# Input projections of a hybrid decoder block: 2x2 block products with seven multiplications in place of eight

## The chip, the cores and the metric

The kernel runs on one core of one Trainium2 chip. The metric is the device time of one execution in microseconds (us); the time of a kernel is the median of its runs. A profiled execution gives, for one run, what each engine did when: TensorE (PE) for matmuls, VectorE (DVE), ScalarE (ACT) and GpSimd (POOL) for the rest, and SyncE (SP), whose queue issues most of the DMA transfers.

## The reference

One decoder block over 2048 positions of 1024 channels, in float32, cut to what matters here:

```python
u = rmsnorm(h, pre_g)                       # [2048, 1024]
z = u @ w_in                                # w_in is [1024, 8192]
xr, zr, q, k, v, za, gm = split(z)          # 1024 channels each, gm 2048
xc = causal_depthwise_conv(xr)              # 4 taps
y_r = rg_lru(xc) * silu(zr)                 # gated linear recurrence over the positions
o = diff_attention(q, k, v, lam)            # 8 heads, two softmaxes of 64 channels each, causal
y_a = rmsnorm(o) * silu(za)
g_r, g_a = split(sigmoid(gm))
m = g_r * (y_r @ w_br_rnn) + g_a * (y_a @ w_br_attn)
h = h + rmsnorm(m @ w_out, post_g)
```

The projection `u @ w_in` is 64 blocks of 128 output channels. Each product of two float32 matrices is done as three float16 matmuls: both sides are scaled by a power of two and split into a high and a low part, and high x high, high x low and low x high are summed in PSUM.

## The kernel before

The kernel has three stages, one after the other, with some overlap at the seams. It is written with a tile framework that adds the waits and puts each engine's instructions in an order by a model of their times, so neighbouring steps interleave.

**The input.** Sixteen tiles of 128 positions are loaded (L240), normalised (`x_stat`, `x_fin`, L252 to L277), split into float16 high and low parts on ACT and on DVE or POOL, and transposed by DMA (L276) into `uT`, which stays in SBUF until the end of attention.

**A weight block** (1024 x 128) is loaded (`w_load`, L145), its sum of squares taken (`w_stat`, L156), a power of two found by a tiny matmul and DVE steps (`w_scale`, L162 to L171), and split into high and low (`w_fin`, L177 on ACT, L178 on DVE). `mm3` (L187 to L194) multiplies a block with 512 positions: 8 parts of the contraction x 3 = 24 matmuls of 512 columns.

**LRU stage.** For each of 8 blocks of 128 channels and each half of the sequence (a half-row), `xr_half` and `zr_half` project x_r and z_r (4 chunks of 24 matmuls), then come the convolution (L324, L327), a split into two float32r parts (`xsplit`), the gate matmuls (`gates`, L351 to L353, twelve of 512 columns), and the recurrence with its scan (`gates2`, L376), then `fin` and `fin2` write the result to DRAM (L416).

**Attention stage.** The work of one head and 128 queries is a unit; there are 128. A unit computes scores (`a_scores`, L814), takes their maximum while DVE copies them out of PSUM (L826, L830), exponentials on ACT (`a_exp`, L851), combines the two softmaxes (`a_comb`, L874 on DVE, L876 on ACT, L877 on POOL), transposes the result by DMA (`pt`, L880), and two units later (`LAG`) multiplies it with v (`a_pv`, L897). Between the units stand groups of projection matmuls as filler, in an order written out as a list (`fills`, L743 to L770): k and q of a chunk (`g_k`, `g_q`, 24 matmuls each, whose outputs are split by `split16`, L667 and L668, and laid out by DMA from SBUF to SBUF, ten transfers a chunk), v and z_a (`g_va`, L711) and the merge gates (`g_gm`, L726 to L729, whose results go to DRAM). How many groups a unit gets is set by its size (L941 to L948).

**Branch stage.** The two branch products (L1094), the merge with the gates read back from DRAM (L1098 to L1108), the output projection (L1125) and the last norm.

## Time and profile before

| | us |
|---|---|
| runs of before: median (lowest to highest of 3) | 2504.65 (2502.78 to 2508.94) |
| span of the profiled execution, first to last instruction | 2506.1 |
| PE busy in it | 2353.1 |
| DVE busy in it | 1548.4 |
| ACT busy in it | 1224.6 |
| POOL busy in it | 679.7 |

The profiled execution has a span of 2506.1 us of its own; its own time with what lies around the span is not listed apart from the three runs, so the span is compared with their median. In a row of a group stands: line, engine, operation, what is written from what, shape and count, then the busy time of all of them together with the mean time of one in ns, then how long the engine was idle before them and who ended that idle time. Matmuls are pipelined: the listed 379 ns of one is longer than the distance from one to the next.

### The profile page before, as it was taken

Reading aid. Unit: us, or ns where it says so; the run is one execution under the profiler, and the core shown is the slowest. Engines: PE = TensorE matmul, PEld = TensorE weight load, DVE = VectorE, ACT = ScalarE, POOL = GpSimd, SP = SyncE. Lnnn points to the kernel's source line nnn. Section 1 sums busy time; section 2 is a strip of 40 time slices with the busy share of each in tenths; the row PEclk is TensorE's granted clock in tenths of the full one; section 3 lists DMA queues with packets and bytes.
Section 4 is the critical chain, followed back from the end, with each engine's and each line's share of the span. In section 5 each row is a group of like instructions: output and inputs, shape, how many; then the busy total and the mean of one; then the engine's idle time right before and its main releaser. Section 6 shows DMA issues by size and latency. Waiting matters only on the chain. (4 is left out here: it accounts for less than half of the span.)

```text
span 2506.1 us, 41430 instructions
## 1 busy us (share of the span) xinstructions
PE 2353.1 (94%) x15240; PEld 1355.3 (54%) x15240; DVE 1548.4 (62%) x4316; ACT 1224.6 (49%) x2156; POOL 679.7 (27%) x415
## 2 busy tenths in 40 slices
PE   6789999999998999998998999999999899999998
PEld 5344444465665665665665655655655444444443
DVE  8877667668658566667567478468467244633323
ACT  5555545456547546556456457356456244312211
POOL 3443334212222212222222222223123133322211
PEclk9899999999999999999999999999999999999999
DMA  9511111235444534635535445445445854743202
GB/s 244 104 43 48 46 42 34 76 81 119 108 96 111 113 84 108 127 82 113 115 84 114 103 96 118 95 90 124 95 90 115 251 177 135 239 148 118 84 17 101
DMA packets 541323, 268.73 MB, mean 107 GB/s; under 512 B 370504, under 2 KB 518016, under 8 KB 541120
## 3 DMA queue, kind: packets, MB, share of 16 engines
q1 hardware_dynamic: 538144, 256.74, 42.6%
q0 software_dynamic: 2816, 9.08, 1.2%
q8 instruction: 119, 1.95, 0.3%
q14 instruction: 84, 0.69, 0.1%
q10 hardware_dynamic: 160, 0.27, 0.0%
HBM read 110.79 MB, written 41.94 MB: 61 GB/s over the span
## 5 line engine op out<-in xcount | busy, mean ns | idle before, releaser
L192 PEld LDWEIGHTS <-w 128*128 128x128 f16 x5040 | 475.9, 100 | 576.5 <-issue 89.2
L192 PE MATMUL mm<-uT,w 128*128 128x512 f16 x3072 | 705.1, 383 | 12.9 <-ACT gm L728 8.9
L877 POOL TENSOR_TENSOR e<-e,e 128x1024 f16<-128x1024 f32 (+2 forms) x192 | 317.0, 1666 | 970.6 <-ACT e L876 487.0
L851 ACT ACTIVATE e<-e,nb,sc_h 128x1024 f32<-128x1024 f32 (+7 forms) x384 | 376.1, 980 | 160.8 <-DVE nb L845 125.6
L826 DVE TENSOR_SCALAR_CACHE_REDUCE e<-sc 128x1024 f32<-128x1024 f32 (+7 forms) x352 | 305.2, 880 | 134.9 <-PE sc L814 122.3
L192 PE MATMUL ps<-uT,w 128*128 128x512 f16 (+1 forms) x1968 | 354.4, 345 | 26.1 <-ACT xr L318 17.7
L711 PE MATMUL mm<-wva,uT 128*128 128x256 f16 x3072 | 352.7, 275 | 3.3 <-DVE st L668 2.6
L1094 PE MATMUL psb<-yt,w 128*128 128x512 f16 x1536 | 332.9, 379 | 2.0 <-ACT w L177 1.5
L711 PEld LDWEIGHTS <-uT 128*128 128x128 f16 x3072 | 301.5, 99 | 48.8 <-issue 2.9
L814 PE MATMUL sc<-K,Q 128*128 128x512 f16 (+3 forms) x1280 | 287.2, 351 | 19.9 <-DVE e L826 13.8
L897 PE MATMUL o<-V,pt 128*128 128x128 f16 x3264 | 224.5, 222 | 38.4 <-DMA pt<-e 38.1
L1094 PEld LDWEIGHTS <-w 128*128 128x128 f16 x1536 | 149.1, 98 | 184.9 <-issue 3.9
L897 PEld LDWEIGHTS <-pt 128*128 128x128 f16 x3264 | 200.0, 99 | 72.8 <-DMA pt<-e 46.5
L876 ACT ACTIVATE e<-e 128x1024 f16<-128x1024 f32 (+2 forms) x192 | 150.1, 802 | 143.1 <-DVE e L874 118.5
L814 PEld LDWEIGHTS <-Q 128*128 128x128 f16 x1280 | 119.6, 99 | 133.2 <-issue 20.2
L874 DVE SCALAR_TENSOR_TENSOR e<-e,rs,e 128x1024 f32<-128x1024 f32 (+2 forms) x192 | 190.0, 1017 | 2.2
L1125 PE MATMUL psf<-wo,m 128*128 128x512 f16 x720 | 155.7, 379 | 0.0
L156 ACT ACTIVATE jk<-wst 128x1024 bf16<-128x1024 f32 x80 | 84.2, 1052 | 138.7 <-DMA wst<-in_w_in_dram 102.6
L1125 PEld LDWEIGHTS <-m 128*128 128x128 f16 x768 | 75.1, 98 | 90.6
L1098 DVE SCALAR_TENSOR_TENSOR t<-gt,psb 128x512 f32<-128x512 f32 x64 | 43.8, 686 | 120.2 <-PE psb L1094 100.1
L1148 ACT ACTIVATE jk<-psf 128x1024 bf16<-128x1024 f32 x15 | 15.4, 1024 | 134.0 <-PE psf L1125 69.4
L717 DVE SCALAR_TENSOR_TENSOR V<-mm,V 128x256 f16<-128x256 f32 x64 | 26.9, 421 | 85.7 <-ACT V L716 85.6
(247 smaller groups left out, 2417.3 us busy)
## 6 DMA issues: line engine op xcount, KB each, us to landing
wst<-in_w_in_dram SPq DMA_DIRECT2D x64, 512.0 KB, 4.5
xt<-in_x_dram SPq DMA_DIRECT2D x32, 512.0 KB, 4.5
gm_d<-gm SPq DMA_DIRECT2D x64, 256.0 KB, 2.7
gt<-gm_d SPq DMA_DIRECT2D x32, 512.0 KB, 3.8
K<-st SPq DMA_DIRECT2D x128, 64.0 KB, 2.0
Q<-st SPq DMA_DIRECT2D x64, 128.0 KB, 2.4
Q<-st SPq DMA_DIRECT2D x128, 64.0 KB, 2.1
ya_d<-yT SPq DMA_DIRECT2D x64, 128.0 KB, 2.0
```

What stands on the lines that cost most here:

```text
L156: nc.scalar.activation(jk, w.st, AF.Square, accum_out=ss)
L192: nc.tensor.matmul(ps, w.t[:, a, k, :], uT[:, b, k, c0:c0 + n], start=(i == 0), stop=(i == 3 * KD - 1))
L711: nc.tensor.matmul(ps[:, j, :], uT[:, a, k, s0:s0 + 128], wt[:, b, k].rearrange("p t f -> p (t f)"), start=(i == 0), stop=(i == 3 * KD - 1))
L814: nc.tensor.matmul(ps[:, x * 128:x * 128 + m], Qt[h, t // 4][:, v, ci, q0:q0 + 128], K[:, ci, 0:m], start=(v == 0), stop=(v == 1))
L826: nc.vector.tensor_scalar(out=ev[:, 0:m], in0=ps[:, 0:m], scalar1=1.0, scalar2=None, op0=ALU.mult, op1=ALU.max, accum_out=u.mx[:, ci, col: ...
L851: nc.scalar.activation(ev[:, 0:nb * 128], ev[:, 0:nb * 128], AF.Exp, bias=nb_[:, ci:ci + 1], scale=sc_h[h], accum_out=u.sm[:, pi, ci:ci + 1])
L874: nc.vector.scalar_tensor_tensor(out=e0[:, 0:m], in0=e1v[:, 0:m], scalar=rs, in1=e0[:, 0:m], op0=ALU.mult, op1=ALU.add)
L876: nc.scalar.activation(e1[:, 0, 0:m], e0[:, 0:m], AF.Copy)
L877: nc.gpsimd.tensor_tensor(out=e1[:, 1, 0:m], in0=e0[:, 0:m], in1=e1[:, 0, 0:m], op=ALU.subtract)
L897: nc.tensor.matmul(o, pt[:, a, kb % 8, :], V[:, kb % 4, b, :], start=(kb == 0 and i == 0), stop=(kb == n - 1 and i == 2))
L1094: nc.tensor.matmul(ps, w.t[:, p, k, :], y_t[b][:, q, k, sl], start=(i == 0), stop=(i == 3 * KD - 1))
L1125: nc.tensor.matmul(pn[n], m16[:, a, j, ms], wo[:, b, j, ns], start=(j == 0 and a == 0 and b == 0), stop=(j == KD - 1 and a == 1))
```

## The change

Four k/q pairs (heads 0 to 3) are projected first, in the plain way: heads 0 and 1 in pieces of 128 positions as the x tiles arrive, heads 2 and 3 in chunks while further input tiles are built. Then come 14 pairs of blocks: x_r with z_r (L, 8 pairs), k with q of heads 4 to 7 (K), and gate blocks 12 to 15 (G, 2 pairs), in the order `S1_ORD`. A pair and half of the sequence form a group. The contraction (1024) is cut in two halves, the pair's two blocks are the two rows, and the half sequence's two chunks of 512 are the two columns of a 2x2 block product, which is done with seven products of 12 matmuls where plain blocks take eight (Winograd's form). For this four sums and differences of weight blocks (S1 to S4) are formed on POOL in each pair, and four of input blocks (T1 to T4) once: x is loaded a second time, combined on DVE and POOL, split and transposed again (`t_load`, `t_build`). Running sums stay in PSUM: bank Y is copied out by ACT (`ev`) before the next product adds to it, and three additions a group are made on DVE (`add_to`).

k and q go to DRAM (`kq_d`) and are loaded from there in attention, six transfers a chunk, four units ahead (`load_kq`). Two of the input's parts (`ub12`) go to DRAM and come back before attention. Attention keeps v, z_a and 12 gate blocks as filler; the first weights of attention are no longer prepared in the LRU stage under a list of their own. Weight blocks are held as two halves in a ring of 10 places (before: 4 whole blocks); some constants (`ACC0`, `SEG_B`, a scale exponent) change with it.

The core of the diff; removed lines are those of the old functions named above.

```diff
+S1_ORD = "L0 K4 L1 K5 L2 G6 L3 K6 L4 G7 L5 L6 L7 K7"
+NGM = 12
...
-        uT = utp.tile([128, 2, KD, S], F16, name="uT")
+        uK = [utp.tile([128, 2, 12, CH], F16, name=f"uK{p}") for p in range(2)]
...
+            pY = lx.enter_context(tc.tile_pool(name="pY", bufs=2, space=PSUM))
+            pX = lx.enter_context(tc.tile_pool(name="pX", bufs=1, space=PSUM))
+            pZ = lx.enter_context(tc.tile_pool(name="pZ", bufs=2, space=PSUM))
+            pG = lx.enter_context(tc.tile_pool(name="pG", bufs=3, space=PSUM))
...
+            def t_build(p, i, ts):
+                a, b = ts
+                for j, t in enumerate((a, b)):
+                    n = p * 8 + j * 4 + i
+                    nc.vector.scalar_tensor_tensor(out=t, in0=t, scalar=rx_t[:, n:n + 1], in1=gb,
+                                                   op0=ALU.mult, op1=ALU.mult)
+                sl = slice(i * 128, (i + 1) * 128)
+                h0, h1 = slice(0, CH), slice(CH, D)
+                nc.vector.tensor_tensor(out=a[:, h0], in0=b[:, h0], in1=a[:, h0], op=ALU.subtract)
+                nc.gpsimd.tensor_tensor(out=b[:, h0], in0=b[:, h1], in1=b[:, h0], op=ALU.subtract)
+                nc.vector.tensor_tensor(out=b[:, h1], in0=b[:, h1], in1=a[:, h0], op=ALU.subtract)
+                nc.vector.tensor_tensor(out=a[:, h1], in0=a[:, h1], in1=b[:, h1], op=ALU.subtract)
+                for src, k0 in ((a, 0), (b, 8)):
+                    u = x_tile(F16, [128, 2, D])
+                    nc.scalar.activation(u[:, 0], src, AF.Copy)
+                    (nc.gpsimd if k0 else nc.vector).tensor_tensor(out=u[:, 1], in0=src, in1=u[:, 0], op=ALU.subtract)
+                    for l in range(2):
+                        nc.sync.dma_start_transpose(out=uM[p][:, l, k0:k0 + 8, sl], in_=u[:, l])
...
+            def p_prep1(r):
+                for w, f in zip(r.w, r.fac):
+                    w_scale(w, gps(1), f)
...
+                nc.gpsimd.tensor_scalar(out=w0.st, in0=w0.st, scalar1=rt, scalar2=None, op0=ALU.mult)
+                r.q = {}
+                for nm, (w, k) in (("A11", (w0, 0)), ("A12", (w0, 4)), ("A22", (w1, 4))):
+                    r.q[nm] = wq_tile()
+                    split_w(r.q[nm], w.st[:, k:k + 4, :], w1.sg)
...
+            def p_prep2(r):
...
+                nc.gpsimd.tensor_tensor(out=a22, in0=a21, in1=a22, op=ALU.add)
+                nc.gpsimd.tensor_tensor(out=a21, in0=a11, in1=a21, op=ALU.subtract)
+                nc.gpsimd.tensor_tensor(out=a11, in0=a22, in1=a11, op=ALU.subtract)
+                nc.gpsimd.tensor_tensor(out=a12, in0=a12, in1=a11, op=ALU.subtract)
+                for nm, src in (("S2", a11), ("S1", a22), ("S3", a21), ("S4", a12)):
+                    r.q[nm] = wq_tile()
+                    split_w(r.q[nm], src, w1.sg)
...
+            def prod(ps, r, p, a, b, start, stop):
+                t, k0 = ublk(p, b)
+                q = r.q[a]
+                i = 0
+                for k in range(4):
+                    for x_, y_ in ((0, 0), (0, 1), (1, 0)):
+                        nc.tensor.matmul(ps, q[:, x_, k, :], t[:, y_, k0 + k, :], start=start and i == 0,
+                                         stop=stop and i == 11, skip_group_check=True)
+                        i += 1
+
+            def ev(src):
+                t = evp.tile([128, CH], F32, tag="Y", name="Y")
+                nc.scalar.activation(t, src, AF.Copy)
+                return t
+
+            def add_to(g, slot, ps, t):
+                dst = c_dst(g, slot)
+                nc.vector.tensor_tensor(out=dst, in0=ps, in1=t, op=ALU.add)
+                c_use(g, slot, dst)
+
+            def g_P1(g):
+                g.Y = pY.tile([128, CH], F32, tag="Y", name="psY")
+                prod(g.Y, g.r, g.p, "A11", "B11", True, True)
+                g.y1 = ev(g.Y)
+
+            def g_P56(g):
+                g.Z = pZ.tile([128, CH], F32, tag="Z", name="psZ")
+                prod(g.Z, g.r, g.p, "S1", "T1", True, True)
+                prod(g.Y, g.r, g.p, "S2", "T2", False, True)
+                g.u2 = ev(g.Y)
+
+            def g_P27(g):
+                X = pX.tile([128, CH], F32, tag="X", name="psX")
+                prod(X, g.r, g.p, "A12", "B21", True, True)
+                add_to(g, 0, X, g.y1)
+                prod(g.Y, g.r, g.p, "S3", "T3", False, True)
+                u3 = ev(g.Y)
+                add_to(g, 3, g.Z, u3)
+
+            def g_P43(g):
+                prod(g.Y, g.r, g.p, "A22", "T4", False, True)
+                c_use(g, 2, g.Y)
+                prod(g.Z, g.r, g.p, "S4", "B22", False, True)
+                add_to(g, 1, g.Z, g.u2)
...
+            for r in plain[2:]:
+                for c in range(NC):
+                    t_build(tn // 4, tn % 4, tl_n)
+                    tn += 1
+                    if tn < 8:
+                        tl_n = t_load(tn // 4, tn % 4)
+                    for f in range(2):
+                        g_plain(r, f, c)
...
+            g_P1(grps[0])
+            for g in grps:
...
+                if nxt:
+                    if g.p == 0:
+                        p_stat(nxt)
+                    else:
+                        p_prep2(nxt)
+                        if n + 2 < len(pairs):
+                            p_load(pairs[n + 2])
+                g_P56(g)
+                tick()
+                g_P27(g)
+                if nxt and g.p == 0:
+                    p_prep1(nxt)
+                if g.n + 1 < len(grps):
+                    g_P1(grps[g.n + 1])
+                tick()
+                g_P43(g)
...
+            def load_kq(h, c):
+                s0 = c * CH
                 t = kp.tile([128, 2, CH], F16, tag="K", name="K")
+                for l in range(2):
+                    nc.sync.dma_start(out=t[64 * l:64 * l + 64], in_=kq_d[0, h, l, :, s0:s0 + CH].rearrange(
+                        "(i p) s -> p i s", i=2))
...
             def chunk_groups(h, c):
-                return [("k", h, c), ("q", h, c), ("va", h, c, 0), ("va", h, c, 1)]
+                return [("va", h, c, 0), ("va", h, c, 1)]
 
-            gms = [("gm", f, c) for f in range(2 * NH) for c in range(NC)]
+            gms = [("gm", f, c) for f in range(NGM) for c in range(NC)]
```

The steps of the recurrence are the same, on the same engines; they are called one, two and three half-groups after their projection (`tick`).

More of the change, by code (lines that the diff above doesn't have):

```diff
@@ new lines, in u_sl, with mm3 @@
+            def u_sl(l, k, c0, n):
+                p, j, o = c0 // HALF, (c0 // CH) % 2, c0 % CH
+                if j == 0:
+                    return uK[p][:, l, k, o:o + n]
+                return uK[p][:, l, 4 + k, o:o + n] if k >= 4 else ub12[p][l][:, k, o:o + n]
+            def mm3(ps, w, c0, n):
+                i = 0
+                for k in range(KD):
+                    for a, b in ((0, 0), (0, 1), (1, 0)):
+                        nc.tensor.matmul(ps, w.at(a, k), u_sl(b, k, c0, n), start=(i == 0), stop=(i == 3 * KD - 1))
+                        i += 1
@@ new lines, with after, tick, c_dst @@
+            later = []
+            clock = [0]
+            def after(n, f):
+                later.append((clock[0] + n, f))
+            def tick():
+                clock[0] += 1
+                for e in [e for e in later if e[0] <= clock[0]]:
+                    later.remove(e)
+                    e[1]()
+            lru = {}
+            def c_dst(g, slot):
+                if g.r.kind == "L" and slot < 2:
+                    if slot == 0:
+                        lru["xr"] = lp.tile([128, HALF + 3], F32, tag="xr", name="xr")
+                    return lru["xr"][:, 3 + slot * CH:3 + (slot + 1) * CH]
+                return stp.tile([128, CH], F32, tag="C", name="C")
@@ L464 @@
             nc.vector.tensor_copy(out=prm, in_=prm_ps)
-            cw = [prm[:, KD * t:KD * (t + 1)] for t in range(4)]
             cb, ba, bx, ap_ = (prm[:, KD * t:KD * (t + 1)] for t in range(4, 8))
@@ new lines, with u_blk @@
+            while later:
+                tick()
+        ubp = utx.enter_context(tc.tile_pool(name="ubp", bufs=1))
+        ub12 = [ubp.tile([128, 2, 4, CH], F16, name=f"ub12{p}") for p in range(2)]
+        for p in range(2):
+            for l in range(2):
+                nc.sync.dma_start(out=ub12[p][:, l].rearrange("p k s -> p (k s)"), in_=b12_d[p, l])
+        def u_blk(l, k, s0, n=128):
+            p, c, o = s0 // HALF, (s0 // CH) % 2, s0 % CH
+            if c == 0:
+                return uK[p][:, l, k, o:o + n]
+            return uK[p][:, l, 4 + k, o:o + n] if k >= 4 else ub12[p][:, l, k, o:o + n]
@@ L594 @@
             ps_m = ax.enter_context(tc.tile_pool(name="ps_m", bufs=2, space=PSUM))
[L597 removed]
+            wl = {}
             wva_t = {}
```

712 lines of the change are left out of this document (387 added, 325 removed).

## Prediction

> **What bounds the kernel now.** I read the page first, for the span and the busy time of each engine, then a table by stage, then what TensorE (PE) waited for, and last the rows of single groups.
>
> ```profile
> span 2506.1 us, 41430 instructions
> PE 2353.1 (94%) x15240; PEld 1355.3 (54%) x15240; DVE 1548.4 (62%) x4316; ACT 1224.6 (49%) x2156; POOL 679.7 (27%) x415
> ```
>
> PE is busy for 94% of the span and idle for 2506.1 - 2353.1 = 153.0 us. The stages show where that idle time lies. The columns are window, length, busy time of PE, PE's weight loads, VectorE (DVE), ScalarE (ACT) and GpSimd (POOL), granted clock, DMA share and GB/s.
>
> ```profile
> 0.00:54.00 54.00, 29.52 (x396) 28.44 (x397) 42.56 (x125) 31.05 (x46) 12.26 (x16) 0.94 1.02 247
> 54.00:104.00 50.00, 35.66 (x290) 22.47 (x287) 46.80 (x92) 21.88 (x30) 27.61 (x20) 0.86 0.85 159
> 104.00:150.00 46.00, 39.27 (x174) 19.37 (x173) 36.84 (x64) 29.15 (x30) 17.54 (x8) 0.96 0.08 24
> 150.00:450.00 300.00, 285.92 (x1281) 138.95 (x1280) 212.36 (x247) 157.09 (x146) 109.94 (x60) 0.97 0.14 44
> 450.00:488.00 38.00, 33.91 (x150) 15.82 (x148) 25.77 (x35) 20.47 (x21) 12.69 (x7) 0.96 0.09 28
> ...
> 600.00:640.00 40.00, 35.08 (x242) 18.83 (x240) 37.20 (x101) 30.04 (x56) 13.97 (x7) 0.96 0.53 127
> ...
> 1963.00:2506.00 543.00, 523.46 (x2428) 236.68 (x2426) 209.98 (x531) 135.06 (x194) 136.29 (x78) 0.99 0.44 140
> ```
>
> ```profile
> 488.00:1963.00 1475.00, 1405.40 (x10532) 893.55 (x10533) 974.11 (x3227) 829.87 (x1692) 363.39 (x228) 0.98 0.49 106
> ```
>
> Idle PE time by stage: opening (0 to 104 us) 24.5 + 14.3 = 38.8; the rest of the LRU stage (104 to 488) 6.7 + 14.1 + 4.1 = 24.9; attention 1475 - 1405.4 = 69.6; branch stage 19.5. So every stage after the opening is bound by PE, and matmuls taken away there are worth their full time as long as nothing else becomes late. The reader should keep two rows. In the opening the DMA share is 1.02, so transfers set the pace. In 600 to 640, inside attention, DVE is busy for 37.20 of 40 us and PE only for 35.08: a stretch where DVE is the late one. PE's waits inside attention say the same:
>
> ```profile
> PE o L897 <- DMA pt<-e: 38.1, 30, 3.2
> PE sc L814 <- DVE e L826: 13.8, 9, 4.4
> ```
>
> PE waits for the transposed softmax weights, the end of a chain through DVE, ACT, POOL and DMA, and for DVE to empty the score banks.
>
> **Term 1: the matmuls removed.** A pair of blocks over half of the sequence took 2 blocks x 2 chunks x 24 = 96 matmuls of 512 columns; seven products of 12 are 84. There are 14 pairs x 2 halves = 28 groups, so 28 x 12 = 336 matmuls go. Their pitch where nothing disturbs PE is in the chain that ended last:
>
> ```profile
> 2249.07 165.76 PE psb L1094 x768
> ```
>
> 165.76 / 768 = 0.2158 us, and 336 x 0.2158 = 72.5 us, certain as long as PE is the bound. It is a small net of large moves: 16 k and q blocks and 4 gate blocks leave the attention stage, where they were the filler between units, and 4 plain pairs and 6 product pairs enter the first stage. The terms below are therefore changes of idle time, stage by stage.
>
> **Term 2: the opening.** Before, three half-rows were computed as x tiles arrived; now four k and q blocks over the whole sequence are, and two more pairs follow while the differences of the input (T1 to T4) are built.
>
> ```profile
> 17.95 0.26 PE L192 MATMUL ps<-uT,w 128*128 128x128 f16 x1 [2.90 <-DMA uT<-u]
> ```
>
> PE has 8 blocks x 96 x 0.2158 = 165.7 us of work here, from 18 us on, and then the first product group (84 x 0.2158 = 18.1 us) before the second half's T is needed: 202 us. The DMA has, from the shapes in the code: x 8.4 MB, its transposes 8.4, x again for T 8.4, T's transposes 8.4, k and q to DRAM 8.4, weights of six pairs 6.3, two of the input's parts to DRAM 2.1, the gain 0.5: 50.9 MB. At the first row's 247 GB/s and share 1.02, that is 242 GB/s at full share, 210 us: 8 us late. With 18 us of start and some 14 us of chain latency for the first T that makes 40 us idle against 38.8: **+1 us**. Bounds: nothing but the start idle, 20 us, is -19. At the second row's rate, 159 / 0.85 = 187 GB/s, the DMA takes 272 us, 70 us late: 90 us idle, +51. I take the first row's rate since its mix of loads and transposes is the nearer one.
>
> **Term 3: the product stage.** The gate matmuls of the LRU are unchanged in number; twelve of them lie between these two rows:
>
> ```profile
> 244.40 0.58 PE L351 MATMUL ps<-xh,gwh 128*128 128x512 f32 x1
> ...
> 247.40 7.94 PE L192 MATMUL ps<-uT,w 128*128 128x512 f16 x36
> ```
>
> 3.0 us a half-row. PE's work is 28 x 84 x 0.2158 + 16 x 3.0 = 556 us. At the idle share of 150 to 450, 14.08 / 300 = 4.7%, that gives 27 us idle. New is a tight hand-over: the running sum in bank Y is copied out by ACT before the next product may add to it, and two of the three copies in a group have only one product (12 x 0.2158 = 2.6 us) of other PE work ahead. The copy itself is like this row, and what ACT may be doing when it comes is like the other two:
>
> ```profile
> L667 ACT ACTIVATE st<-mm 128x512 f16<-128x512 f32 x64 | 37.6, 587 | 66.4 <-PE mm L192 57.3 <-PE tot L162 4.9 <-DMA Q<-st 3.2
> L156 ACT ACTIVATE jk<-wst 128x1024 bf16<-128x1024 f32 x80 | 84.2, 1052 | 138.7 <-DMA wst<-in_w_in_dram 102.6 <-POOL wst L150 30.1 <-DMA ya_d<-yT 5.6
> ```
>
> ```profile
> ACT sq L369 <- DVE sq L363: 31.0, 12, 4.9
> ```
>
> 0.59 us fits four times into 2.6 us; behind one long operation it still fits; but ACT stood up to 4.9 us at the head of its queue waiting for DVE's sq, and a copy behind that is late. ACT was busy 157.09 of 300 us, so most copies find it free: 56 hand-overs x 0.1 us = 6. Idle 33 against 24.9: **+8**. Bounds: none late, +2; each late by one ACT operation, 56 x 1.05 = 59, +61. The three additions a group (DVE, from PSUM) and the seven half-splits a pair hide beside the products; what they do to DVE is the fourth rival.
>
> **Term 4: into attention.** Before, head 0's k and q projections covered the preparation of its v and z weights, and PE's waits at the seam were short:
>
> ```profile
> 487.67 0.28 PE L711 MATMUL mm<-wva,uT 128*128 128x256 f16 x1 [0.60 <-ACT wva L177]
> ...
> 490.26 0.27 PE L814 MATMUL sc<-K,Q 128*128 128x128 f16 x1 [1.19 <-DMA Q<-st]
> ```
>
> ```profile
> wst<-in_w_in_dram SPq DMA_DIRECT2D x64, 512.0 KB, 4.5
> ```
>
> Now the first PE work of attention is v and z themselves, in tiles that stand where the first stage's lie; only the last group's products can cover them. If the loads are early, a split on ACT and DVE and its semaphores remain: **+4 us**. Bounds: 0 if all is covered; two loads of 4.5 us, a square of 1.05 and two splits behind the last product, some 13 us. The Trainium skill (TensorE: Matmul & The Clock Gate, Part 1) says that an idle window of about 3.4 us halves PE's clock; by it a seam of 4 us costs some 1.7 us more, an estimate from that page. The granted 0.86 of 54 to 104 us, beside 14.3 us of idle, agrees in kind.
>
> **Term 5: attention.** Its PE work falls by more than a quarter, DVE's hardly. The first two rows are those of the projection line L192 alone, in the attention window and behind it.
>
> ```profile
> 488.00:1963.00 1475.00, 657.76 (x2873) 279.31 (x2874) 0.98 0.49 106
> 1963.00:2000.00 37.00, 24.58 (x104) 10.48 (x102) 0.95 0.94 299
> ```
>
> ```profile
> L668 DVE SCALAR_TENSOR_TENSOR st<-mm,st 128x512 f16<-128x512 f32 x64 | 43.8, 685 | 54.9 <-ACT st L667 54.9
> ...
> L178 DVE SCALAR_TENSOR_TENSOR w<-wst,w_sg_agm,w 128x1024 f16<-128x1024 f32 x16 | 23.8, 1487 | 0.8 <-ACT w L177 0.7
> ```
>
> Of its 2873 matmuls there, 12 gate blocks keep 12 x 96 = 1152, less the 104 that run after 1963: 1048. So 1825 go; at 0.2158 they are 394 us, at their own 657.76 / 2873 = 0.229 they are 418, say 405: PE's 1405 becomes 1000. DVE loses the split of k and q (43.8) and 20 weight splits of 1.49 (30): 974 becomes 900. DVE's work over PE's goes from 0.69 to 0.90; in 600 to 640 it was 37.20 / 35.08 = 1.06, with PE idle for 4.92 of 40 us, 12.3%, where the stage as a whole idled for 69.6 / 1475 = 4.7%. I read the idle share off the straight line between these two: 4.7 + (0.90 - 0.69) / (1.06 - 0.69) x 7.6 = 9.0%, and 1000 x 0.09 / 0.91 = 99 us against 69.6: **+29**. Bounds: 4.7% gives 50 us, -20; 12.3% gives 140 us, +71.
>
> On the queues: before, SP issued ten copies a chunk that laid k and q out, behind their splits; now six loads from DRAM, issued four units ahead, and SP has less to issue between the transposes of the softmax weights. I cost this at nothing; without the lead it would be a wait like the 1.19 us above, once a chunk. The branch stage keeps its matmuls and its 19.5 us; its weight splits come in halves, behind PE: 0.
>
> **Sum.** -72.5 + 1 + 8 + 4 + 29 = -30.5, so 2506.1 - 30.5 = 2475.6 us in a profiled execution. The profiled execution of before was 1.5 us above the median of its runs, 2504.65; taken off, that is **2474 us**. With every term at its low end the changes add up to -110, with every term at its high end to +124.
>
> **Rivals.** *Everything hides* (2415 us): the hand-overs cost nothing and attention keeps 4.7%: -72.5 + 1 + 2 + 0 - 20 = -89.5. For it speaks that PE reached 95% of 1475 us already, against it the 600 to 640 row. Chance 0.15.
>
> *DVE paces attention* (slower). If the whole stage runs as 600 to 640 does, because too little filler lies between a unit's scores and its product with v, the idle time is 140 us and the sum 2474 + 71 - 29 = 2516 us. It decides from an idle share of 11.4%, where attention's idle time has grown by 60 us and the gain is gone. For it: the two waits quoted at the start, both on that chain; DVE would need 900 of 1140 us. Against it: the 40 us are one dense stretch, between quieter ones in which DVE catches up. Chance 0.15.
>
> *The opening waits for DMA* (2474 + 50 = 2524 us), if the transposes run at the second row's rate. Against it: in 54 to 104 us DVE was busy for 46.80 of 50 us and held up what the transposes read. Chance 0.07.
>
> *DVE paces the LRU groups*. In 150 to 450 us there were 1281 / 108 = 11.9 half-rows, so DVE had 212.36 / 11.9 = 17.9 us each. Three additions of the kind of the first row below (2.1 us) and three more half-splits a pair (0.9 a half-row) make 20.9 us, beside PE's 84 x 0.2158 + 3.0 = 21.1. POOL gets a scaling like the third row and four half-size additions and subtractions like the second for each pair, (1.86 + 4 x 1.20) / 2 = 3.3 us a half-row, and some DVE operations with two inputs in SBUF take far longer than their like: the fourth row has a median of 1282 ns and a longest of 3150 ns.
>
> ```profile
> L1098 DVE SCALAR_TENSOR_TENSOR t<-gt,psb 128x512 f32<-128x512 f32 x64 | 43.8, 686 | 120.2 <-PE psb L1094 100.1 <-PE tot L162 9.4 <-issue 4.7
> ...
> L1108 POOL TENSOR_TENSOR m<-t,m 128x512 f16<-128x512 f32 x32 | 38.5, 1204 | 116.5 <-ACT m L1107 116.5
> ...
> L324 POOL TENSOR_SCALAR xc<-xr,prm 128x1024 f32<-128x1024 f32 x16 | 29.7, 1859 | 56.7 <-ACT xr L318 53.3 <-DVE xt L266 3.3
> ```
>
> ```profile
> L327 DVE SCALAR_TENSOR_TENSOR xc<-xr,prm,xc x48: 1270/1282/3150, 73.4 to 456.6; 128x1024 f32<-128x1024 f32 x48
> ```
>
> If each new POOL operation holds DVE up for its whole length, a half-row takes DVE 24.2 us, 3.1 more than PE, and 16 of them 50 us: 2524. The Trainium skill (SBUF — State Buffer, Who interferes with whom) has it as a rule: a DVE instruction with two SBUF inputs and a GpSimd instruction that reads SBUF exclude each other, and whichever starts second waits for all of the other. The long ones of the fourth row would fit it; that POOL was the cause is not shown by this row. What speaks against the price is the order of the pairs: k/q and gate groups, which need DVE for about 8 of 18 us, stand between most LRU groups. Chance 0.05.
>
> *The change is not what it says*: fewer than 336 matmuls go. The page's count would show it; I give it no chance of its own, since the loops write out 84.
>
> **How the numbers follow.** My forecast, 2440 to 2497 us, has 0.50; an outcome between it and before, 2497 to 2512, has 0.08. Faster by over 0.3% (below 2497; about what a measurement of this kernel can tell from no change) is 0.50 + 0.15 = 0.65, within 0.3% is 0.08, slower is 0.15 + 0.07 + 0.05 = 0.27. The range for 8 in 10 cuts little from the two sides: 2418, just above the full gain, to 2545, which is DVE pacing attention with half of one of the other two on top.
>
> **What would show it.** Matmuls: 15240 - 336, and in the opening 384 x 4 narrow ones in place of 384 of 512 columns where before 576 took the place of 144: + 1152 - 432, so 15624. With the granted clock a few hundredths under 1 in the first stages, as before: first product at about 215 us, first scores at about 825, first branch matmul at about 1965. PE idle 40 us up to the first product, 33 in the products, 99 in attention, and DVE busy for 0.8 of attention. I am wrong if PE's wait for pt or for score banks in attention adds up to well over 100 us, if the first T comes 30 us or more after PE asks for it, or if PE's waits for ACT's copies of Y show up at the top of the product stage's list.

## The result, and the profile after

| | us |
|---|---|
| after, median (lowest to highest of 4 runs) | 2655.9 (2652.5 to 2662.7) |
| before, median (lowest to highest of 4 runs) | 2506.3 (2502.8 to 2508.9) |
| after / before, 95% interval | 1.060 (1.058 to 1.062) |
| forecast (range) | 2474 (2418 to 2545) |

The change makes the kernel 6.0% slower: 150 us lost where 30 were expected to be won. The head of the page of after:

```profile
span 2654.7 us, 43007 instructions
...
PE 2334.8 (88%) x15624; PEld 1359.0 (51%) x15624; DVE 1758.0 (66%) x4640; ACT 1322.2 (50%) x2430; POOL 854.1 (32%) x517
```

The matmul count is the forecast one. PE is idle for 2654.7 - 2334.8 = 319.9 us, where it was 153.0 before. By stage (opening up to the first product, products, seam up to the first scores, attention, branch; columns as in the prediction):

```profile
0.00:243.00 243.00, 182.24 (x1934) 133.60 (x1934) 147.73 (x351) 89.27 (x136) 55.60 (x47) 0.92 0.88 198
243.00:938.00 695.00, 599.03 (x2570) 271.26 (x2570) 468.77 (x670) 335.30 (x483) 301.34 (x161) 0.93 0.19 56
938.00:977.00 39.00, 13.18 (x101) 10.56 (x100) 20.40 (x36) 16.71 (x23) 7.16 (x6) 0.65 0.41 116
977.00:2133.00 1156.00, 1031.97 (x8677) 714.33 (x8678) 906.77 (x3038) 743.13 (x1576) 355.89 (x226) 0.97 0.60 127
2133.00:2655.00 522.00, 508.40 (x2344) 229.26 (x2342) 214.34 (x546) 137.79 (x216) 134.12 (x77) 0.99 0.42 132
```

Idle PE time is 60.8, 96.0, 25.8, 124.0 and 13.6 us. The product stage stands out twice. PE idles for 96 us, and its clock is 0.93, so the 599 us that it is busy are longer than the 556 us of work: 28 x 84 x 0.2158 for the products and 48 for the LRU's gate matmuls. No engine there is busy for more than 70% besides PE. What PE waited for in that stage, from behind its first product on (engine, what, released by; total, count, longest):

```profile
PE psX L382 <- DVE xr L393: 22.1, 4, 7.4
PE psY L382 <- ACT Y L388: 19.4, 12, 4.2
PE psZ L382 <- DVE C L393: 14.7, 3, 6.8
PE gps L554 <- POOL xl L524: 11.7, 6, 2.7
PE psY L382 <- DVE g L507: 7.2, 3, 4.1
```

No single wait explains 96 us. Of the 95 us that the whole list adds up to, 55 end with DVE and 19 with ACT's copies of Y, and POOL's xl stands there too. The timeline shows what a long wait does to PE afterwards:

```profile
830.65 4.90 PE L382 MATMUL psX<-uK,wq 128*128 128x512 f16 x12 [7.36 <-DVE xr L393]
```

These twelve matmuls take 4.90 us, 0.41 each, where an undisturbed one takes 0.2158. The Trainium skill (TensorE: Matmul & The Clock Gate, Part 1) says that an idle window of about 3.4 us halves the clock; this row agrees. The wait cost 7.36 us and another 2.3 behind it.

### The profile page after: what moved, and what is told of

Read it like the earlier page. It is cut to its first block, busy times and chain, and to the rows that moved or that the text cites. A ratio compares the mean times of both kernels' runs of the same rounds, so it can differ in the third digit from the quotient of the medians.

```text
span 2654.7 us, 43007 instructions
## 1 busy us (share of the span) xinstructions
PE 2334.8 (88%) x15624; PEld 1359.0 (51%) x15624; DVE 1758.0 (66%) x4640; ACT 1322.2 (50%) x2430; POOL 854.1 (32%) x517
## 5 line engine op out<-in xcount | busy, mean ns | idle before, releaser
L1091 ACT ACTIVATE e<-e,nb,sc_t 128x1024 f32<-128x1024 f32 (+7 forms) x384 | 376.2, 981 | 160.6 <-DVE nb L1085 111.1
L382 PEld LDWEIGHTS <-wq 128*128 128x128 f16 x2352 | 233.4, 101 | 397.0 <-issue 130.8
L1336 PE MATMUL psb<-yt,wq 128*128 128x512 f16 x1536 | 337.9, 383 | 5.8 <-DMA yt<-yr_d 2.6
L947 PE MATMUL mm<-wva,uK 128*128 128x256 f16 x2304 | 293.9, 276 | 29.1 <-ACT wva L179 24.1
L1137 PE MATMUL o<-V,pt 128*128 128x128 f16 x3264 | 236.9, 224 | 66.2 <-DMA pt<-e 65.7
L382 PE MATMUL psY<-uM,wq 128*128 128x512 f16 x1008 | 246.3, 394 | 19.7 <-ACT Y L388 19.4
L947 PEld LDWEIGHTS <-uK 128*128 128x128 f16 x2304 | 225.1, 99 | 66.9 <-ACT wva L179 24.2
L1336 PEld LDWEIGHTS <-wq 128*128 128x128 f16 x1536 | 150.3, 99 | 189.8 <-issue 9.5
L1114 DVE SCALAR_TENSOR_TENSOR e<-e,rs,e 128x1024 f32<-128x1024 f32 (+2 forms) x192 | 205.1, 1096 | 1.8
L966 PE MATMUL mm<-uK,wq 128*128 128x512 f16 x864 | 201.6, 381 | 0.4 <-ACT gm L970 0.4
L966 PEld LDWEIGHTS <-wq 128*128 128x128 f16 x1152 | 111.9, 99 | 133.1 <-issue 12.9
L163 DVE CAST w_s<-w_ss 128x1 bf16<-128x1 f32 x80 | 12.1, 153 | 163.6 <-ACT jk L161 163.5
L382 PE MATMUL psY<-uK,wq 128*128 128x512 f16 x336 | 85.4, 398 | 27.8 <-ACT wq L179 14.2
```

The costliest lines, as they stand in the source:

```text
L382: nc.tensor.matmul(ps, q[:, x_, k, :], t[:, y_, k0 + k, :], start=start and i == 0, stop=stop and i == 11, skip_group_check=True)
L947: nc.tensor.matmul(ps[:, j, :], u_blk(a, k, s0), wt[:, b, k].rearrange("p t f -> p (t f)"), start=(i == 0), stop=(i == 3 * KD - 1))
L966: nc.tensor.matmul(ps, wt[k // 4][:, a, k % 4, :], u_blk(b, k, c * CH, CH), start=(i == 0), stop=(i == 3 * KD - 1))
L1091: nc.scalar.activation(ev[:, 0:nb * 128], ev[:, 0:nb * 128], AF.Exp, bias=nb_[:, ci:ci + 1], scale=sc_t[:, h:h + 1], accum_out=u.sm[:, pi, ...
L1114: nc.vector.scalar_tensor_tensor(out=e0[:, 0:m], in0=e1v[:, 0:m], scalar=rs, in1=e0[:, 0:m], op0=ALU.mult, op1=ALU.add)
L1137: nc.tensor.matmul(o, pt[:, a, kb % 8, :], V[:, kb % 4, b, :], start=(kb == 0 and i == 0), stop=(kb == n - 1 and i == 2))
```

## Experiments

Times are in us. "Products" is the time from the first product to the last, "seam" from there to the first scores, "attention" from those to the first branch matmul. after, eight_products, seven_combined and eight_combined have four runs each, the other rows one; product stages of single runs differ by up to 24 us where an edit did not touch it (t_ring, weights_ahead and opening_untied against after), so a difference of that size is read as an effect only where another kernel bears it out.

| kernel | first product | products | seam | attention | time |
|---|---|---|---|---|---|
| after | 243.5 | 690.8 | 42.3 | 1156.3 | 2655.9 |
| eight_products | 210.1 | 653.3 | 29.2 | 1155.8 | 2576.9 |
| no_recurrence | 282.2 | 516.9 | 8.9 | 1171.7 | 2487.6 |
| no_weight_sums | 240.8 | 661.9 | 42.7 | 1162.5 | 2630.6 |
| t_ring | 245.4 | 680.5 | 42.0 | 1165.9 | 2656.8 |
| recurrence_unlinked | 255.6 | 703.2 | 15.4 | 1168.8 | 2651.0 |
| unlinked_less_dve | 243.3 | 602.9 | 12.1 | 1159.0 | 2540.4 |
| unlinked_less_pool | 244.5 | 593.7 | 12.1 | 1161.8 | 2534.4 |
| unlinked_less_act | 250.2 | 694.9 | 15.5 | 1172.1 | 2640.9 |
| weights_ahead | 238.9 | 677.2 | 41.6 | 1171.3 | 2639.4 |
| order_end | 245.7 | 746.7 | 9.2 | 1152.4 | 2678.9 |
| gates_to_attention | 241.4 | 652.5 | 43.4 | 1229.2 | 2679.0 |
| opening_untied | 238.4 | 666.6 | 41.7 | 1174.3 | 2630.5 |
| sums_on_dve | 243.1 | 659.1 | 42.2 | 1169.3 | 2622.3 |
| all_on_dve | 243.2 | 618.0 | 40.0 | 1159.8 | 2583.0 |
| eight_all_on_dve | 211.3 | 628.2 | 29.1 | 1152.6 | 2543.5 |
| seven_combined | 236.1 | 662.3 | 9.0 | 1151.1 | 2585.8 |
| eight_combined | 208.8 | 634.4 | 1.8 | 1172.3 | 2545.8 |

My first theory was *late queues*: the recurrence's steps wait for each other at the heads of the in-order queues of DVE, ACT and POOL, and the product hand-overs stand behind them. Its rivals: *hand-over* (the seven-product form's own copies and additions make PE wait) and *weight sums* (POOL's new work is late or holds DVE up).

**eight_products.** Staging, order and queues of after, plain products:

```diff
-                g_P56(g)
...
-                g_P27(g)
...
+                prod(ps, g.r, g.p, f"A{f}1", f"B1{c}", True, False)
+                prod(ps, g.r, g.p, f"A{f}2", f"B2{c}", False, True)
...
-                    t_build(tn // 4, tn % 4, tl_n)
```

> The 14 pairs with eight plain products of 12 matmuls (no T, no weight sums, no running sum that is copied out); order, queues, rings and the recurrence as after the change. PE's work in the product stage is 28 x 96 x 0.2158 + 48 = 628 us (with seven: 555.8, of 694.5 us). Late queues (the recurrence and its short rings hold up the engines that empty PSUM): the stage still loses 80 to 110 us and takes 710 to 740. Hand-over (the seven-product form itself, its copies and additions, makes PE wait): the loss falls to about 30 us, the stage takes 650 to 670 and is shorter than with seven. Without the T builds the first product should come at about 206 us in place of 243.5 under both. Total: late queues 2640 to 2670, hand-over 2570 to 2590.

Ratio to before 1.029 (1.027 to 1.032), 79 us faster than seven. The stage took 653.3 us for 628 us of PE work, as *hand-over* said; the first product came at 210, so the T builds cost the opening some 33 us. (This version also leaves out the weight sums; where they alone are left out, in no_weight_sums, the first product came 3 us earlier.)

```profile
210.00:864.00 654.00, 635.63 (x2908) 296.95 (x2907) 335.59 (x527) 278.77 (x383) 171.09 (x92) 0.99 0.17 53
```

DVE is busy for 133 us less than with seven, POOL for 130 less; how much of DVE's 133 is work and how much waiting this row does not tell.

**no_recurrence.**

```diff
-                    after(1, lambda: lru_conv(r, p))
-                    after(2, lambda: lru_gates(r, p))
-                    after(3, lambda: lru_scan(r, p))
+                    lru.pop("xr")
...
+                            nc.gpsimd.dma_start(out=yr_d[:, r.i, :, cs].rearrange("l p s -> p l s"), in_=yz)
```

> Leaves out the convolution, the LRU gates, the recurrence and its output (zeros are written to the DRAM tensor that the branch stage reads); the seven products, their copies and the weight preparation stay. PE's work in the product stage is 28 x 84 x 0.2158 = 507 us. Late queues: the loss of 139 us goes almost wholly, stage 520 to 550 us, and the seam of 25 us shrinks to about 5. Hand-over: 90 us of loss or more stay, stage 600 or more. Weight sums on POOL: about half stays, 570 or more.

```profile
282.00:799.00 517.00, 513.58 (x2395) 232.63 (x2396) 202.61 (x454) 196.33 (x321) 114.05 (x71) 0.99 0.21 63
```

516.9 us for 507.6 of work, a little better than *late queues* forecast: with nothing else on the engines, the seven-product form costs next to nothing, and *hand-over* alone is out. So the form by itself loses 9 us, the recurrence beside eight plain products 25; together they lose 135. (The opening came out 39 us longer here; its instructions stand in another order, and I did not follow that.)

**no_weight_sums.** The five POOL operations of a pair's weights are left out.

```diff
-                nc.gpsimd.tensor_scalar(out=w0.st, in0=w0.st, scalar1=rt, scalar2=None, op0=ALU.mult)
...
-                nc.gpsimd.tensor_tensor(out=a22, in0=a21, in1=a22, op=ALU.add)
-                nc.gpsimd.tensor_tensor(out=a21, in0=a11, in1=a21, op=ALU.subtract)
-                nc.gpsimd.tensor_tensor(out=a11, in0=a22, in1=a11, op=ALU.subtract)
-                nc.gpsimd.tensor_tensor(out=a12, in0=a12, in1=a11, op=ALU.subtract)
```

> Leaves out the scaling and the four sums of weights on POOL in each pair (the splits then take the unsummed weights, so the products are of other numbers); all else as after the change. Weight sums on POOL: the product stage falls from 694.5 by 50 us or more, and the mean of the convolution's DVE step falls from 1750 ns to about 1490. Late queues: it falls by 10 to 30 us only, as POOL's queue frees the transfers of the recurrence earlier. Hand-over: no change.

The stage fell by 29 us, which is what *late queues* forecast (10 to 30) and not the 50 of *weight sums*; the mean of the convolution's DVE step fell from 1750 to 1390 ns, further than *weight sums* said (1490). The sums are at most a part.

**recurrence_unlinked.**

```diff
-                    nc.vector.scalar_tensor_tensor(out=xc, in0=xr[:, t:t + HALF], scalar=r.cwz[:, t:t + 1],
-                                                   in1=xc, op0=ALU.mult, op1=ALU.add)
+                    nc.vector.scalar_tensor_tensor(out=jD, in0=K, scalar=cb[:, b:b + 1],
+                                                   in1=K, op0=ALU.mult, op1=ALU.add)
```

All other wide steps of the recurrence are edited alike, with jD for DVE, jP for POOL and jA for ACT.

> The recurrence keeps all its operations in number, shape and engine, but they read a constant tile and write one throw-away tile per engine (the LRU's values are not computed): the same work, without the chain from engine to engine and without the product stage's tiles as its input. The product stage had 695 us with the recurrence and 517 without it (48 of it gate matmuls). Chain (a waiting step of the recurrence stands at the head of DVE's, ACT's or POOL's queue and the hand-overs stand behind it): the stage loses at most 30 us, 585 us or less. Amount of work (DVE and POOL have so much that hand-overs queue anyway): 640 us or more.

703.2 us, as the second half of the expectation had it. The chain can go and nothing is won: *late queues* falls in the form in which I stated it. The waits only moved, to the weights' preparation (33 us for the small steps of `w_stat`, 36 for the splits). What counts is the amount of work, although no engine is full. That left the question whose.

**unlinked_less_dve, unlinked_less_pool, unlinked_less_act.** The unlinked kernel, with one engine's wide operations left out; one line of each:

```diff
-                nc.vector.tensor_tensor_scan(jD, K, K, 0.0, ALU.mult, ALU.add)
```

```diff
-                nc.gpsimd.tensor_tensor(out=jP, in0=K, in1=K, op=ALU.mult)
```

```diff
-                nc.scalar.activation(jA, K, AF.Sqrt, scale=0.25)
```

> The unlinked recurrence without its wide operations on DVE (three taps, a copy, two products, the scan and its product a half-row, the maximum a block; 254 us in all); its ACT, POOL and PE operations stay, and so does all weight work. The product stage took 703 us with them (255.6 to 958.8). If the amount of DVE work is what PE waits behind, the stage falls to 590 us or less; if POOL (or the sharing of memory between POOL and DVE) or ACT is, it stays at 640 or more.

> The unlinked recurrence without its four POOL operations a half-row (154 us), and without the weights' scaling and sums on POOL (some 140 us): POOL does nothing wide in the product stage, DVE and ACT keep all their operations. If DVE is late because it and POOL hold each other up, DVE's operations become shorter (the taps 1686 ns to about 1270, the tiny scale steps 600 to about 160) and the stage falls from 703 to 610 us or less; if the amount of DVE's own work decides, it stays at 650 or more.

> The unlinked recurrence without its seven wide ACT operations a half-row (four gate tanh, exponential, tanh, square root; some 90 us): DVE and POOL keep theirs. If ACT, which also copies bank Y out, is where the hand-overs queue, the stage falls from 703 to 620 us or less; if DVE or POOL is, it stays at 660 or more.

First products at 243.3, 244.5 and 250.2; the stage took 602.9, 593.7 and 694.9 us, against 703.2. ACT is out. DVE and POOL each give back 100 us or more (unlinked_less_dve between its two forecasts, unlinked_less_pool as the first half of its expectation said), which looks like two causes until DVE's busy time is read. The stage's row of recurrence_unlinked, then of unlinked_less_pool:

```profile
255.60:958.80 703.20, 596.93 (x2571) 271.68 (x2572) 488.52 (x641) 342.44 (x491) 310.15 (x166) 0.93 0.18 55
```

```profile
244.50:838.20 593.70, 568.07 (x2572) 266.84 (x2572) 377.24 (x653) 342.98 (x494) 28.35 (x35) 0.98 0.23 68
```

With POOL nearly silent DVE does the same operations, give or take a dozen, in 377 us in place of 489: 111 us of DVE's busy time was waiting for POOL. It lies in the wide operations (the taps' mean went from 1686 to 1281 ns); the tiny scale steps, which the expectation put at 600 ns, took 153 in recurrence_unlinked already. How the waiting looks in after, on DVE and POOL (the lines of other engines are left out):

```profile
396.52 2.36 POOL L524 TENSOR_TENSOR xl<-xc,xh 128x1024 fp32r<-128x1024 f32 x1 [5.68 <-DVE xh L523]
396.96 1.95 DVE L511 COPY xr<-halo 128x3 f32<-128x3 f32 x1
398.82 0.68 DVE L507 SCALAR_TENSOR_TENSOR g<-g,C 128x512 f32<-128x512 f32 x1
...
409.72 1.89 POOL L562 TENSOR_TENSOR sq<-a 128x1024 f32<-128x1024 f32 x1 [10.84 <-ACT a L559]
409.75 1.88 DVE L176 SCALAR_TENSOR_TENSOR w_cz<-w_iv_p,cu 128x1 f32<-128x1 f32 x1
```

A copy of three columns takes 1.95 us and a product of one column 1.88; their median durations are 162 and 154 ns. The first ends at 398.91, POOL's subtraction at 398.88; the second at 411.63, POOL's product at 411.61. Each started second, waited for all that was left of the other, and kept the rest of DVE's queue waiting. POOL is held up too: without DVE's wide work (unlinked_less_dve) its own in the stage went from 310 to 260 us. The Trainium skill (SBUF — State Buffer, Who interferes with whom) gives this as a rule, for DVE operations with two SBUF inputs and for copies in a two-port mode; both rows agree, though the trace does not say in which mode the copy ran.

**sums_on_dve, all_on_dve, eight_all_on_dve** ask whether this decides in the kernel itself. Nothing is left out; POOL's work goes to DVE:

```diff
-                nc.gpsimd.tensor_tensor(out=a22, in0=a21, in1=a22, op=ALU.add)
+                nc.vector.tensor_tensor(out=a22, in0=a21, in1=a22, op=ALU.add)
...
-                nc.gpsimd.tensor_tensor(out=xl, in0=xc, in1=xh.bitcast(F32), op=ALU.subtract)
+                nc.vector.tensor_tensor(out=xl, in0=xc, in1=xh.bitcast(F32), op=ALU.subtract)
```

> The weights' scaling and four sums a pair are computed on DVE instead of POOL; nothing is left out. DVE gets 14 x (0.7 + 4 x 0.7) = 49 us more of its own work, POOL loses 130. If the two engines hold each other up, the product stage falls from 691 us (243.5 to 934.3) to 630 to 670 and DVE's busy time there grows by less than 30 us; if DVE's own load decides, the stage grows by 10 to 40 us.

> As sums_on_dve, and the recurrence's four POOL operations a half-row are on DVE too, some 16 x 4.4 = 70 us more of its own work, so that POOL does nothing wide in the product stage and DVE all. Holding up: DVE's busy time stays near 470 us although it does 120 us more work, and the stage falls to 620 to 660. DVE's own load: the stage grows by 60 us or more.

> The eight-product version with the recurrence's POOL operations on DVE. There PE lost 25 to 30 us in 653 and DVE was busy for 336 us, POOL for 171, so both theories have slack: the stage stays within 10 us of 653, and DVE's busy time stays within 30 us of 336 although it does 70 us more work, if the two held each other up there too.

The whole stage of all_on_dve, and its convolution steps beside those of after:

```profile
243.20:861.20 618.00, 572.10 (x2561) 265.91 (x2562) 488.34 (x802) 332.25 (x480) 24.12 (x30) 0.97 0.21 63
...
L519 DVE SCALAR_TENSOR_TENSOR xc<-xr,cwz,xc 128x1024 f32<-128x1024 f32 x48 | 61.2, 1276 | 0.3
```

```profile
L519 DVE SCALAR_TENSOR_TENSOR xc<-xr,cwz,xc 128x1024 f32<-128x1024 f32 x48 | 84.0, 1750 | 2.8 <-POOL xc L516 2.0
```

DVE takes over some 120 us of work, its busy time goes from 468.8 to 488.3, and the stage is 73 us shorter; sums_on_dve alone gave 32. DVE's own load, which grew, is not what decided; the overlap with POOL was. One rival is weakened, not excluded: all_on_dve also takes POOL's slower operations out of the way of the recurrence and of the weights' splits. Against it stand recurrence_unlinked, where the chain is gone and the stage is no shorter, and unlinked_less_dve, where POOL keeps all its operations and the stage takes 602.9 us.

The control left both its bounds (10 us for the stage, 30 for DVE): eight products won 25 us in the stage and DVE's busy time there grew by 34 for 70 us of work, so the overlap cost something with slack too. With it gone, seven products take 618.0 us and eight 628.2: of the 72.5 us of removed matmuls 10 arrive, and the opening takes 32 back. The stage of eight_all_on_dve, and PE's two longest waits in that of all_on_dve:

```profile
211.30:839.50 628.20, 626.02 (x2906) 296.21 (x2905) 368.97 (x589) 280.17 (x383) 19.93 (x28) 1.00 0.18 54
```

```profile
PE psY L382 <- ACT Y L388: 18.4, 9, 4.9
PE gps L553 <- DVE xh L523: 15.0, 3, 8.5
```

Eight products now lose nothing; seven still take 62 us more than their 556 us of work, 46 of them idle time of PE. So the overlap is 73 of the 135 us that the product stage of after loses. The cause of the rest is open: no run tells DVE's own load (488 of 618 us) from the hand-over of bank Y.

**t_ring, weights_ahead, opening_untied** look at the opening: the T tiles' split parts in a ring of their own; the weights ahead of the T builds; both, with the plain pairs' outputs on ACT's queue.

```diff
-                    u = x_tile(F16, [128, 2, D])
+                    u = x_tile(F16, [128, 2, D]) if p else e0p.tile([128, 2, D], F16, tag="u16", name="u16")
...
+                if i == 12:
+                    for f in range(2):
+                        q_fin(plain[3], f)
...
-            k_out(r, f, c, ps, nc.sync)
+            k_out(r, f, c, ps, nc.scalar)
```

> The split parts of the first four T tiles go into the opening's own ring of four instead of the ring of five x tiles, and that ring's memory is handed over after them. If the ring of five is what makes a T build take 18 us, the first four come 10 to 12 us apart and the first product starts at 210 to 225 us in place of 243.5; if DVE, ACT or the transfers set the 18 us, it stays within 6 us of 243.5. The later stages should not change.

> The scale and the splits of the fourth plain pair's weights are put ahead of the T builds, and those of the first product pair two chunks earlier; the T builds stay. If PE's two waits of 15.9 and 14.2 us in the opening come from weight preparation that stands on DVE and ACT behind T builds which wait for their x loads, both waits fall below 5 us and the first product comes at 212 to 222 us in place of 243.5. If the T chain itself paces the opening, the wait moves to the first products and they start within 6 us of 243.5.

> Three edits of the opening at once: the weights ahead of the T builds, the split parts of the first four T tiles in the opening's own ring, and the outputs of the plain pairs issued from ACT's queue, so that the x loads of the next T tile do not stand behind them on SP. Each of the first two alone moved the first product by under 5 us. If the opening is a ring of queues that wait for each other (x loads behind outputs, weights behind T builds, outputs behind weights), all three together bring the first product from 243.5 to 210 to 222 us; if the transfers themselves are the limit, it stays above 232. The product stage keeps its 695 us.

First product at 245.4, 238.9 and 238.4: none of the three edits brought it near 215. For t_ring and weights_ahead the time is that of the second half of the expectation (within 6 us). For opening_untied its second half gives the number, but the trace does not show that transfers are the limit: the first four T builds came 12 us apart on average, as wanted, the rest 17 to 18, and PE still stood for 13 us behind a small weight step on DVE:

```profile
209.77 5.28 PE L439 MATMUL psP<-b,wq 128*128 128x512 f16 x12 [13.08 <-DVE w_tot L169]
```

That the T builds cost some 33 us is shown by eight_products. What sets their pace is open: the ring is part of it for the first four, and these three edits do not settle the rest.

**order_end** and **gates_to_attention**:

```diff
-S1_ORD = "L0 K4 L1 K5 L2 G6 L3 K6 L4 G7 L5 L6 L7 K7"
+S1_ORD = "L0 K4 L1 K5 L2 L3 K6 L4 L5 G6 L6 L7 K7 G7"
```

```diff
-S1_ORD = "L0 K4 L1 K5 L2 G6 L3 K6 L4 G7 L5 L6 L7 K7"
-NGM = 12
+S1_ORD = "L0 K4 L1 K5 L2 L3 K6 L4 L5 L6 L7 K7"
+NGM = 16
```

> Only the order of the pairs: L0 K4 L1 K5 L2 L3 K6 L4 L5 G6 L6 L7 K7 G7, so that four groups without a recurrence stand behind the last LRU pair. If the seam of 39 us is the end of the recurrence (the v and z weights' splits stand behind its output splits), the time from the last product to the first scores falls from 42 us to 15 or less; if it is the weights' own loading and splitting or the return of the parked input, it stays at 35 or more. The product stage, with three runs of two LRU pairs in place of one run of three, stays within 15 us of 695.

> All 16 gate blocks stay with attention and the two gate pairs leave the product stage: 4 x 96 matmuls more in attention, 82.9 us of PE work at 0.2158, and 4 groups of 18.1 us fewer before it. If DVE and the softmax chain pace attention, the added filler is partly free and attention with its tail of gates grows by 45 to 65 us; if PE is the bound there, by 80 to 88. The product stage loses 72 us of PE work and falls by 72 to 90.

The seam of after, and the place where its wait went in order_end:

```profile
963.20 0.61 PE L947 MATMUL mm<-wva,uK 128*128 128x256 f16 x2 [24.07 <-ACT wva L179]
```

```profile
963.57 5.28 PE L382 MATMUL psZ<-uM,wq 128*128 128x512 f16 x12 [21.52 <-DVE C L393]
```

The seam fell to 9 us, as forecast, but the products grew by 56, where 15 was the bound: the wait stands in them, 21.5 us of it in one wait near the recurrence's end. It is a backlog, and another order only moves it. It is not the overlap with POOL: in all_on_dve the seam is still 40.0 us. gates_to_attention says the same from the other side: 72 us of matmuls left the products, and they became only 38 shorter, where 72 to 90 were forecast. In attention 82.9 us of filler cost 73, above the one forecast and below the other; since that stage differs by up to 23 us between kernels that do not touch it (1151 to 1174), this says that PE's work there is paid for the larger part, and no more.

**seven_combined, eight_combined, before_on_dve**, all with an interval. In seven_combined and eight_combined the pairs stand in this order:

```diff
-S1_ORD = "L0 K4 L1 K5 L2 G6 L3 K6 L4 G7 L5 L6 L7 K7"
+S1_ORD = "L0 K4 L1 L2 K5 L3 L4 G6 L5 L6 K6 L7 G7 K7"
```

> opening_untied and all_on_dve together, and the pairs in the order L0 K4 L1 L2 K5 L3 L4 G6 L5 L6 K6 L7 G7 K7, so that two pairs without a recurrence stand at the end. If the three causes add up: first product at 235 to 240 us, product stage 600 to 625 us, last product to first scores 15 us or less in place of 40, attention and branch as after the change: 2535 to 2560 us in all, still slower than before (2506). If the order brings back the backlog that it brought in order_end, the stage takes 640 or more and the total is 2565 or more.

> eight_all_on_dve with the same order of the pairs. First product at 211 us, product stage 625 to 640, seam 15 or less: 2510 to 2535 us in all. Seven products are worth their place only if seven_combined is faster than this one; from the stages so far (seven lose 32 us in the opening and win 10 in the product stage) it is 15 to 30 us slower.

> The kernel before with the recurrence's four POOL operations a half-row on DVE; nothing else changed. Its LRU stage lost 25 us of PE time in 384 with DVE busy for 0.7 and POOL for 0.37 of it, so there is slack: within 8 us of 2506, rather a little faster than slower.

Ratios to before: seven_combined 1.033 (1.031 to 1.035), eight_combined 1.016 (1.014 to 1.018). In both, the order took the seam away and brought the backlog back in the seven-product stage (662 us), as the second half of the expectation had it; with eight, where DVE has room, the stage stayed at 634, though the 27 us of the seam were not won in the whole (attention came out 20 longer, within the spread named above). Seven products lose by 40 us even here. eight_combined was forecast at 2510 to 2535 us and took 2545.8. Both are slower than the kernel before.

before_on_dve, the kernel before with four words changed (L324, L338, L362, L370: `nc.gpsimd` to `nc.vector`), took 2476.1 us, ratio 0.989 (0.987 to 0.991): faster than both kernels, by more than I expected. Its row for the window that the prediction read its 4.7% idle share from:

```profile
150.00:450.00 300.00, 299.09 (x1382) 147.30 (x1381) 254.09 (x309) 166.45 (x154) 7.99 (x14) 1.00 0.14 46
```

PE idles for 0.9 us in place of 14.1, its clock is 1.00 in place of 0.97, and 1382 matmuls fit where 1281 did. The first scores come at 467.7 instead of 488.4. What I took for the idle share of a stage bound by PE went away almost wholly when POOL's part of the recurrence moved to DVE.

## Why the prediction was wrong, point by point

**Term 1** was right in count, and in time where nothing is late: 516.9 us for 507.6 of work in no_recurrence. Its condition, "as long as PE is the bound", failed.

**Term 2** (opening, +1): idle time grew by 22, first product at 243.5 in place of 215. The transfers came out as summed (0.88 of 243 us is 214, for 210), but they were not what ended last. PE's two long waits there end with steps of the weights' preparation:

```profile
168.61 8.28 PE L439 MATMUL psP<-uK,wq 128*128 128x512 f16 x28 [15.95 <-DVE w_tot L169]
...
243.55 1.03 PE L382 MATMUL psY<-uK,wq 128*128 128x512 f16 x2 [14.17 <-ACT wq L179]
```

I gave the T chain 14 us once, for its first tile; the builds follow each other at 18 us (DVE's first subtraction of each: 122.5 to 248.4 us, seven steps), against 10.4 us of PE work each, and cost some 33 us (eight_products). Which of their steps the weights stood behind is not shown.

**Term 3** (products, +8) is the step that failed: idle time 96 in place of 33, which is +71 where the upper bound was +61, and PE slow behind the waits, for which the sum had no term (599 us busy for 556 of work). Forecast from the first product to the first scores: 610 us; measured 733, which is 123 of the 182 us by which the forecast missed. I priced the hand-overs by what ACT does, and took over the idle share of before. What ended more than half of the waiting was DVE, held up by POOL; without the overlap the stage is 73 us shorter, and the whole kernel too (2583.0 us). The mechanism was in my fourth rival, POOL holding DVE up, at a chance of 0.05 and 50 us. The failed argument was the one against it: that k/q and gate groups "need DVE for about 8 of 18 us" and so leave room. The recurrence's steps run up to one and a half groups behind their products, and land in them. Four stretches of after, about two LRU halves and two k/q halves:

```profile
337.10:367.90 30.80, 22.45 (x91) 9.63 (x90) 13.98 (x33) 16.87 (x23) 8.68 (x5) 0.88 0.16 44
367.90:394.50 26.60, 21.80 (x85) 9.04 (x85) 16.32 (x23) 11.96 (x20) 8.32 (x7) 0.82 0.35 109
394.50:415.50 21.00, 21.00 (x100) 10.30 (x99) 14.59 (x26) 10.80 (x15) 7.36 (x4) 1.00 0.04 13
415.50:441.10 25.60, 22.34 (x95) 10.04 (x94) 19.75 (x20) 7.27 (x12) 17.19 (x7) 0.93 0.16 49
```

In the second k/q half DVE is busy for 19.75 us and POOL for 17.19, beside 18.1 us of products. Over the stage 468.8 us of DVE and 301.3 of POOL stand in 691, both with the time in which one waits for the other; what cannot overlap must queue, though neither is full. That the mechanism also lengthens tiny operations, the weights' scale steps among them, was not in my sum. The 62 us that all_on_dve still loses in this stage are a second miss of this term, with its cause open; the hand-overs of Y, which I put at 6 us, are 18 of them.

**Term 4** (seam, +4, bounds 0 to 13): one wait of 24.07 us, beyond the bound. My bound counted loads and splits, not the backlog in front of them.

**Term 5** (attention, +29): first scores to first branch matmul took 1156 us against 1140 forecast. DVE's share came out at 0.78 for 0.8, idle time at 124 for 99, inside its bounds, and PE's waits for pt came to 65.7 us, where they had been 38.1:

```profile
PE o L1137 <- DMA pt<-e: 65.7, 57, 4.5
```

With 37.3 us for the score banks that is 103, at the edge of the sign I had named. Still *DVE paces attention*, my main slower case, is not what happened as stated: it would have needed 140 us of idle time, and it was the product stage that sank the change. But it was not far: the idle share was 10.7%, where 11.4% would have used up the gain. The remaining 11 us are in the branch stage; 5 of them are 24 gate matmuls that run behind its start, the cause of the rest is open.

Of the signs that I named, PE's waits for the copies of Y did show near the top of the product stage's list: 19.4 us here, 1.9 in no_recurrence, 18.4 in all_on_dve. So they need the recurrence beside them, but not POOL's work: they are a smaller loss of their own beside the overlap.

## What to carry to other kernels

A stage is not bound by one engine because the others are busy for less than 70%: add DVE and POOL together where both work on SBUF, and see whether the sum fits into the stage. A sum that fits is no proof of safety: in eight_products 336 + 171 us stood in 653, and moving POOL's work still won 25. Look at the shortest operations for it; a three-column copy of 2 us shows at once what an average hides. Before work is moved to an idle POOL, try it on DVE: here that was worth 1.1% in the kernel before, while removing an eighth of the stage's product matmuls was worth 10 us there and cost 32 in the opening.

## What the runs showed of the hardware that I had not expected

- DVE's busy time with the same operations: 489 us beside POOL's 310 us of work, 377 without it. A POOL operation with two inputs of 128 x 1024 float32 took 1.9 to 2.8 us in after (means of three lines), 2.0 with DVE's wide work left out (unlinked_less_dve); DVE does the same in 1.22 (all_on_dve).
- Taking POOL's work onto DVE raised DVE's busy time by 20 us for about 120 us of work, and by 34 for 70 where the two had met less.
- After waits of 6 to 7 us, 12 matmuls of 512 columns took 4.9 to 5.1 us in place of 2.6, so the longest waits of the product stage cost a third to two fifths again.
